# An order written by a model: memory-path transfers, first byte and arrival enter the model up to a given time

## The chip, the cores and the metric

One Trainium2 chip, of which the kernel uses one core. The metric is device time in microseconds of one execution; the median of three runs of the kernel before is 947.36 us (947.36 to 947.47).

## The reference

Two layers on 256 positions of width 1024, all in float32. Each layer is

```python
h = rmsnorm(x, ffn1_norm[i])
x = x + 0.5 * swiglu(h, ffn1_w_gate[i], ffn1_w_up[i], ffn1_w_down[i])      # 1024 -> 2816 -> 1024
h = rmsnorm(x, mix_norm[i])
q_s, k_s, v_s, q_m = jnp.split(h @ w_in[i], ...)                           # 1024 -> 3*768 + 256
k_m, v_m = jnp.split(rmsnorm(mem, mem_norm[i]) @ w_mem_kv[i], 2, axis=-1)  # 256 memory rows
o_m = memory_attention(rmsnorm(q_m), rmsnorm(k_m), v_m)                    # 4 heads of 64
o_s = chunked_rel_attention(...) if i % 2 == 0 else diff_attention(...)    # 12 heads, or 6 double ones
x = x + jnp.concatenate([o_s, o_m], axis=-1) @ w_out[i]
h = rmsnorm(x, ffn2_norm[i])
x = x + 0.5 * swiglu(h, ffn2_w_gate[i], ffn2_w_up[i], ffn2_w_down[i])
```

So there are four feed-forward parts and two attention parts: feed-forward, attention, feed-forward (layer 0), then the same for layer 1.

## The kernel before, in words

**The arithmetic.** TensorE works on fp32r operands. To keep float32 accuracy each operand is split in a high part (a cast) and a low part (the rest), and each product takes three matmuls: high with high, high with low, low with high (`dense`, L542, L545, L548). Weights come as blocks of 128 x 2048 floats (1 MB) into one of three `raw` buffers. ACT casts them to `hi` (`split_hi`, L367) and DVE subtracts to get `lo` (`split_lo`, L385), into one of four split buffers. Some products use seven products in place of eight, on sums of blocks (`wsum`, L379; the matmul groups `pair_m` and `m`).

**A feed-forward part.** Eleven groups of 256 hidden columns, each with two blocks that hold gate and up columns (`gu` banks), then eleven blocks of the down projection (`acc` banks). After a group `evac` takes it out: ACT's silu (L728), DVE's product (L731) and a 32 x 32 transpose into `hb` (L739). The rest of the transpose is a trip through DRAM: `hd` from `hb` (L745) and back as `hr` (L751), both issued on SyncE. Then `hr` is split to `ht`, the left operand of the down projection.

**Attention.** The input projection in five column groups (`pj` banks), a norm of each head (`qkn`, L1049), TensorE transposes (`qktp`), scores (`S`), softmax, transposes of the probabilities, values (`AV`), and the output projection. Layer 0 also holds, ahead of it, the projection of the memory rows. These rows go through DRAM too (`through_dram`, L1064, and `from_dram`, L1069: tiles `md` and `mr`), as do the memory keys (`kd` and `kr`).

**What sets the order.** No scheduler reorders anything: each engine runs its instructions in the order in which the program emits them. The order comes from a small model, `Flow`, that runs while the program is written. It has a clock `now`, which a matmul of 512 columns moves by `T_MM` = 0.216 us, and a time at which each of ACT, DVE and GpSimd gets free. Pieces of work are generators that yield the model time, or the condition, at which they may go on. When TensorE's next matmul needs something, the model lets time pass until it is there, and emits on the way whatever other work has become ready. Semaphores on the chip still hold each instruction until its operands are there, so a wrong model costs time, and nothing else.

Three generators bring in the weights, in the background. `loader` issues a block's transfers on SyncE's queue as soon as a `raw` buffer is free in the model (L321), and writes down when it takes the block to have arrived. `split_hi` emits the casts of a block after that time, when ACT has nearly no backlog in the model or TensorE needs the block; `split_lo` does the same on DVE and frees the `raw` buffer. `dma_free` is the model's time at which the queue has finished: it grows by 3.0 per block, and by small amounts for the first loads of x and the small parameters. In the kernel before no other transfer is in it. The trips through DRAM have fixed delays of their own (3.0, 2.0 and 6.5 around `hd` and `hr`).

Of the kernel before, what the change touches and what calls it, by code (L numbers as in the profile page):

```python
# [167 lines left out]
def kernel(  # L168
# [13 lines left out]
    flow = Flow()  # L182
# [28 lines left out]
    def load_x(tb, hf):  # L211
        nc.sync.dma_start(out=xs[tb][:, hf * 512:(hf + 1) * 512],
                          in_=x[0, tb * P:(tb + 1) * P, hf * 512:(hf + 1) * 512])
# [86 lines left out]
    dma_free = [3.25]  # L300
    slow = [0.0]
    LAT = 1.5
    at = [0]

    def add_raw(parts):
        chunks.append(Chunk(parts))
        return chunks[-1]

    def add_chunk(parts, uses=8, w=1):
        return Item([add_raw(parts)], uses, w)  # L310

    def loader():
        for i, c in enumerate(chunks):
            yield lambda: raw_left[0] > 0
            raw_left[0] -= 1
            c.raw = wraw.tile([P, 2048], F32, tag="raw", name=f"raw{i}")
            dma_free[0] = max(dma_free[0], flow.now)
            n = len(c.parts)
            lat = LAT + slow[0] if i > 1 else 0.6
            for j, (dst, src) in enumerate(c.parts):  # L320
                (nc.scalar if i == 0 and j == 1 else nc.sync).dma_start(out=dst(c.raw), in_=src)  # L321
                dma_free[0] += 3.0 / n
                if i < 2 and j % 2:
                    for q in range((j - 1) * 4 // n, (j + 1) * 4 // n):
                        c.block[q] = dma_free[0] + lat
                if i == 0 and j == 1:
                    table_hint(AF.Silu)
                    load_x(1, 0)
                    dma_free[0] += 0.75
            c.arrive = dma_free[0] + lat  # L330
            c.block = [t or c.arrive for t in c.block]
            if i == 1:
                for tb in range(2):
                    load_x(tb, 1)
                    dma_free[0] += 0.75
            if i > 4 and late_done[0] < len(late_loads):
                dst, src = late_loads[late_done[0]]
                late_done[0] += 1
                nc.sync.dma_start(out=dst, in_=src)
                dma_free[0] += 0.3  # L340
# [371 lines left out]
    def ffn(l, nm, xt, gc_next):  # L712
# [6 lines left out]
        def evac(g, ps, end, gives=None):  # L719


            hb = None
            for tb in range(2):
                yield lambda: end[tb] is not None and xt.rt[tb] is not None
                yield end[tb]
                yield g2.has(3)
                sil = g2.take([P, 256], F32, "sil")
                nc.scalar.activation(sil, ps[tb][:, 0:256], AF.Silu, scale=xt.r[tb])  # L728
                yield flow.act(256)
                h = g2.take([P, 256], F32, "h")  # L730
                nc.vector.scalar_tensor_tensor(out=h, in0=ps[tb][:, 256:512], scalar=xt.r[tb], in1=sil,  # L731
                                               op0=ALU.mult, op1=ALU.mult)
                t = flow.dve(256, 0.06)
                g2.give()
                (gives or (banks, banks))[tb].give()
                if hb is None:
                    hb = g2.take([P, 4, 2, 2, 32], F32, "hb")
                yield t
                nc.vector.transpose(out=hb[:, :, tb].rearrange("p b f j -> p f b j"),  # L739
                                    in_=h.rearrange("p (f b i) -> p f b i", f=2, b=4))  # L740
                t = flow.dve(256, 0.05)
                g2.give()
            yield t
            hd = dram.tile([4, 32, 4, P], F32, tag="hd", name="hd")
            nc.sync.dma_start(out=hd.rearrange("a i b x -> (a i) (b x)"), in_=hb.rearrange("p b t f j -> p (b t f j)"))  # L745
            yield flow.now + 3.0
            g2.give()
            yield flow.now + (8.0 if (l, nm) == (0, 1) and g < NG - 3 else 2.0)
            yield g2.has()
            hr = g2.take([P, 4, P], F32, "hr")  # L750
            nc.sync.dma_start(out=hr, in_=hd.rearrange("a i b x -> (i b) a x"))  # L751
            yield flow.now + 6.5
            src = hr.rearrange("p a (c j) -> p c a j", c=4)
            if g in sv:
                yield from seven_forms(g, src)
                return
            yield g4.has()
            ht = g4.take([P, 2, 4, P], F32R, "ht")
            hi, lo = (ht[:, i].rearrange("p c (a j) -> p c a j", a=4) for i in range(2))
            nc.scalar.copy(out=hi, in_=src)  # L760
            yield flow.act(512)
            nc.vector.tensor_sub(lo, src, hi.bitcast(F32))
            t = flow.dve(512)
            g2.give()
            hts[g], htt[g] = ht, t

        def seven_forms(g, src):


            yield lambda: g4.left >= 2 and g2.left >= 4 and (sv.index(g) < 2 or prog[0] >= sv[1])  # L770
            ht = [g4.take([P, 8, P], F32R, "h7") for _ in range(2)]
            sf = g2.take([P, 4, P], F32, "sf")
            s1, s2, s3, s4 = (sf[:, j].rearrange("p (a j) -> p a j", a=4) for j in range(4))
            for op, o, x, y in ((nc.vector.tensor_add, s1, src[:, 2], src[:, 3]), (nc.vector.tensor_sub, s2, s1, src[:, 0]),
                                (nc.vector.tensor_sub, s3, src[:, 0], src[:, 2]), (nc.vector.tensor_sub, s4, src[:, 1], s2)):
                op(o, x, y)
                t = flow.dve(P, 0.06)
            yield t
            view = lambda x: x.rearrange("p c (a j) -> p c a j", a=4)
            parts = ((slice(0, 2), src[:, 0:2], view(ht[0][:, 0:2]), view(ht[1][:, 0:2])),  # L780
                     (slice(2, 3), src[:, 3:4], view(ht[0][:, 2:3]), view(ht[1][:, 2:3])),
                     (slice(3, 7), sf, ht[0][:, 3:7], ht[1][:, 3:7]))
            ts = []
            for js, x, hi, lo in parts:
                nc.scalar.copy(out=hi, in_=x)
                ts.append(flow.act(P * (js.stop - js.start)))
            for (js, x, hi, lo), t in zip(parts, ts):
                yield t
                nc.vector.tensor_sub(lo, x, hi.bitcast(F32))
                t = flow.dve(P * (js.stop - js.start))  # L790
            g2.give(2)
            hts[g], htt[g] = ht, t

        def seven(c, ms):

            flow.until(lambda: hts[c] is not None)
            ht, first, last = hts[c], c == sv[0], c == sv[-1]
            for q, j, m in ((0, 0, 0), (1, 1, None), (2, 6, None), (3, 3, 1), (4, 4, 2), (5, 5, 3), (6, 2, None)):
                ps = ms[m] if m is not None else acc.ps[q // 6][q // 2 % 2 if q < 6 else 0]
                t = dense(ps, ht[0][:, j], ht[1][:, j], lambda: htt[c], dn[c], q,  # L800
                          first and m is not None, last and m is not None)
            g4.give(2)
            return t
# [164 lines left out]
        def down(c, k, tb, hf):  # L968
            sl = slice(hf * 512, (hf + 1) * 512)
            flow.until(lambda: hts[c] is not None)  # L970
            ht = hts[c]
            return dense(acc.ps[tb][hf], ht[:, 0, 2 * tb + k, :], ht[:, 1, 2 * tb + k, :], lambda: htt[c], dn[c], 2 * k + hf,
                         c == 0 and k == 0, k == 1 and c == NG - (2 if split_end and tb == hf == 1 else 1))
# [24 lines left out]
        for c in range(SPLIT):  # L998
            prog[0] = c
            if c in sv:  # L1000
# [3 lines left out]
                t = seven(c, ms)  # L1004
# [15 lines left out]
        for tb in range(2):  # L1020
            flow.spawn(finish(acc, tb, nxt, gc_next, True, (l, nm) == (0, 1)))
            for hf in range(2):
                for c in range(SPLIT, NG - (split_end and tb == hf == 1)):
                    for k in range(2):
                        t = down(c, k, tb, hf)
                if split_end and tb == hf == 1:
                    t = end_sums(t)
# [4 lines left out]
    def table_hint(func):  # L1032
        nc.scalar.activation(dummy, dummy, func)
        flow.act(1, 1.3)
# [27 lines left out]
    def through_dram(src, tag, n):  # L1062
        d = dram.tile([4, 32, 4, P], F32, tag=tag, name=tag, bufs=n)
        nc.sync.dma_start(out=d.rearrange("a i b x -> (a i) (b x)"), in_=src.rearrange("p b t k j -> p (b t k j)"))  # L1064
        return d

    def from_dram(d, name):
        r = g2.take([P, 4, 2, 2, 32], F32, name)
        nc.sync.dma_start(out=r.rearrange("p a t k j -> p a (t k j)"), in_=d.rearrange("a i b x -> (i b) a x"))  # L1069
        return r  # L1070

    def turn_blocks(dst, src):
# [777 lines left out]
```

## Time and profile before

| | |
|---|---|
| median of three runs | 947.36 us |
| the profiled execution | 947.91 us |
| span in its profile | 946.1 us, so 1.8 us lie around it |
| TensorE matmuls (PE) busy | 940.1 us, 99% |
| VectorE (DVE) busy | 830.1 us, 88% |
| ScalarE (ACT) busy | 590.6 us, 62% |
| GpSimd (POOL) busy | 110.2 us, 12% |
| transfers | 206.13 MB, mean 218 GB/s |
| granted TensorE clock | 1.0 |

All times in views of the trace are microseconds from the span's start, and an L with a number is a line of the kernel. PE is TensorE's matmuls, PEld its weight loads, SPq SyncE's queue. A name such as `lo<-raw,hi` is out<-in by the program's tile names. A wait is shown as who waited, then `<-`, then what ended the wait.

### The profile page before, as it was taken

To read this page: it belongs to the slowest core of one execution; us is meant where nothing else is said; L and a number is where in the kernel's file an instruction comes from. 1 tells how busy PE (TensorE), PEld (TensorE's weight loads), DVE (VectorE), ACT (ScalarE), POOL (GpSimd) and SP (SyncE) were. 2 spreads that over 40 slices of the span, in tenths; PEclk is the share of its full clock that TensorE was granted. 3 is DMA by queue.
4 is the path that set the end of the run, shared out by engine and by line. 5 is a ranking of instruction groups with operands and counts; after the bars stand their busy time and mean duration, and the time that the engine had idled before them with its cause. 6 is when DMAs were issued, how large, how long until landed. Compare 5 with 4: busy or idle time off the path is not lost. (4 is left out here: it accounts for less than half of the span.)

```text
span 946.1 us, 13322 instructions
## 1 busy us (share of the span) xinstructions
PE 940.1 (99%) x4456; PEld 773.6 (82%) x4456; DVE 830.1 (88%) x1501; ACT 590.6 (62%) x1126; POOL 110.2 (12%) x160
## 2 busy tenths in 40 slices
PE   9999999999999999999999999999999999999998
PEld 7888888887878888888888888888887788888887
DVE  6989988889787879979889899796999899998995
ACT  6656666677686746647545656563777765655671
POOL 1000038732220000000000000000334100000000
PEclk9999999999999999999999999999999999999999
DMA  9878799788524476887846679775642367589561
GB/s 294 272 228 252 231 324 315 241 263 260 178 90 146 150 250 210 265 287 225 269 146 214 210 237 286 242 249 176 202 130 75 130 222 223 188 251 333 185 220 47
DMA packets 172574, 206.13 MB, mean 218 GB/s; under 512 B 10265, under 2 KB 147290, under 8 KB 172506
## 3 DMA queue, kind: packets, MB, share of 16 engines
q1 hardware_dynamic: 169498, 202.92, 66.9%
q10 hardware_dynamic: 3008, 2.37, 0.8%
q8 instruction: 35, 0.57, 0.3%
q14 instruction: 33, 0.27, 0.1%
HBM read 190.04 MB, written 15.20 MB: 217 GB/s over the span
## 5 line engine op out<-in xcount | busy, mean ns | idle before, releaser
L367 ACT CAST hi<-raw 128x512 fp32r<-128x512 f32 (+1 forms) x466 | 335.6, 770 | 157.3 <-DMA raw<-in_ffn_w_up_dram 53.1
L385 DVE TENSOR_TENSOR lo<-raw,hi 128x512 fp32r<-128x512 f32 (+1 forms) x466 | 393.0, 878 | 28.7 <-ACT hi L367 28.2
L542 PE MATMUL gu<-hi,xh 128*128 128x512 f32 x528 | 206.1, 390 | 0.0
L548 PE MATMUL gu<-hi,xl 128*128 128x512 f32 x528 | 206.0, 390 | 0.0
L545 PE MATMUL gu<-lo,xh 128*128 128x512 f32 x528 | 206.0, 390 | 0.0
L545 PEld LDWEIGHTS gu<-lo,xh 128*128 128x128 f32 x528 | 99.4, 188 | 20.9 <-DVE lo L385 0.4
L542 PEld LDWEIGHTS gu<-hi,xh 128*128 128x128 f32 x528 | 99.6, 189 | 20.5
L548 PEld LDWEIGHTS gu<-hi,xl 128*128 128x128 f32 x528 | 99.4, 188 | 20.6
L548 PE MATMUL acc<-hi,ht 128*128 128x512 f32 x270 | 105.6, 391 | 0.0
L542 PE MATMUL acc<-hi,ht 128*128 128x512 f32 x270 | 105.1, 389 | 0.0
L545 PE MATMUL acc<-lo,ht 128*128 128x512 f32 x270 | 105.1, 389 | 0.0
L367 ACT CAST hi<-wsum 128x512 fp32r<-128x512 f32 x83 | 49.0, 620 | 42.4 <-DVE wsum L379 36.5
L545 PE MATMUL pj<-lo,xh 128*128 128x512 f32 x160 | 63.9, 399 | 0.0
L548 PE MATMUL pj<-hi,xl 128*128 128x512 f32 x160 | 63.8, 399 | 0.0
L542 PE MATMUL pj<-hi,xh 128*128 128x512 f32 x160 | 63.5, 397 | 0.0
L585 POOL TENSOR_TENSOR xr<-v,nhalf 128x1 f32<-128x1 f32 x12 | 9.7, 810 | 427.4 <-DVE v L583 427.4
L545 PEld LDWEIGHTS acc<-lo,ht 128*128 128x128 f32 x270 | 50.7, 188 | 10.6
L548 PEld LDWEIGHTS acc<-hi,ht 128*128 128x128 f32 x270 | 50.7, 188 | 10.4
L542 PEld LDWEIGHTS acc<-hi,ht 128*128 128x128 f32 x270 | 50.7, 188 | 10.3
L385 DVE TENSOR_TENSOR lo<-wsum,hi 128x512 fp32r<-128x512 f32 x83 | 53.7, 678 | 0.0
L728 ACT ACTIVATE sil<-gu,xr 128x256 f32<-128x256 f32 x72 | 33.8, 469 | 21.1 <-PE gu L548 19.6
L585 POOL TENSOR_TENSOR hf<-v,nhalf 128x8 f32<-128x8 f32 (+1 forms) x20 | 33.2, 1659 | 83.2 <-DVE v L583 74.1
(244 smaller groups left out, 1531.7 us busy)
## 6 DMA issues: line engine op xcount, KB each, us to landing
raw<-in_ffn_w_down_dram SPq DMA_DIRECT2D x176, 256.0 KB, 4.5
raw<-in_ffn_w_gate_dram SPq DMA_DIRECT2D x82, 512.0 KB, 4.7
raw<-in_ffn_w_up_dram SPq DMA_DIRECT2D x82, 512.0 KB, 5.2
raw<-in_w_in_dram SPq DMA_DIRECT2D x32, 512.0 KB, 4.9
hd<-hb SPq DMA_DIRECT2D x44, 256.0 KB, 4.9
hr<-hd SPq DMA_DIRECT2D x44, 256.0 KB, 4.9
raw<-in_w_out_dram SPq DMA_DIRECT2D x8, 1024.0 KB, 4.9
raw<-in_w_mem_kv_dram SPq DMA_DIRECT2D x4, 1024.0 KB, 8.5
```

Source lines behind the costliest of these rows:

```text
L367: nc.scalar.copy(out=it.part(0, q, w), in_=src())
L385: nc.vector.tensor_sub(it.part(1, q, w), src(), it.part(0, q, w).bitcast(F32))
L542: nc.tensor.matmul(out=ps, lhsT=xh, rhs=wh, start=start, stop=False)
L545: nc.tensor.matmul(out=ps, lhsT=xh, rhs=wl, start=False, stop=False)
L548: nc.tensor.matmul(out=ps, lhsT=xl, rhs=wh, start=False, stop=stop)
L585: nc.gpsimd.tensor_tensor(out=dst, in0=v[:, :n], in1=nhalf[:, :n], op=ALU.pow)
L728: nc.scalar.activation(sil, ps[tb][:, 0:256], AF.Silu, scale=xt.r[tb])
```

## The change

While the model's clock is below `FULL` = 600:

- the issue of `hd`, `hr` and of the trips of memory rows and memory keys now moves `dma_free`: to 1.7 after now if the queue is idle (the time to the first byte), and 0.8 further (`carry`);
- a weight block starts on the queue 1.7 after its issue at the earliest, in place of at once;
- a weight block counts as arrived 1.9 after its last byte's time, in place of 1.5 (the first two blocks keep their 0.6).

From 600 on the model is as before. No instruction of the kernel is changed; only the order in which they are emitted can be.

```diff
+    FULL = 600.0
+
+    def carry(t):
+        if flow.now < FULL:
+            dma_free[0] = max(dma_free[0], flow.now + 1.7) + t
...
-            dma_free[0] = max(dma_free[0], flow.now)
+            dma_free[0] = max(dma_free[0], flow.now + (1.7 if flow.now < FULL else 0.0))
             n = len(c.parts)
-            lat = LAT + slow[0] if i > 1 else 0.6
+            lat = (1.9 if flow.now < FULL else LAT) + slow[0] if i > 1 else 0.6
...
             nc.sync.dma_start(out=hd.rearrange("a i b x -> (a i) (b x)"), in_=hb.rearrange("p b t f j -> p (b t f j)"))
+            carry(0.8)
             yield flow.now + 3.0
...
             nc.sync.dma_start(out=hr, in_=hd.rearrange("a i b x -> (i b) a x"))
+            carry(0.8)
             yield flow.now + 6.5
...
     def through_dram(src, tag, n):
         d = dram.tile([4, 32, 4, P], F32, tag=tag, name=tag, bufs=n)
         nc.sync.dma_start(out=d.rearrange("a i b x -> (a i) (b x)"), in_=src.rearrange("p b t k j -> p (b t k j)"))
+        carry(0.8)
         return d

     def from_dram(d, name):
         r = g2.take([P, 4, 2, 2, 32], F32, name)
         nc.sync.dma_start(out=r.rearrange("p a t k j -> p a (t k j)"), in_=d.rearrange("a i b x -> (i b) a x"))
+        carry(0.8)
         return r
```

## The prediction

> **What bounds the kernel now.** I read four views in this order: the page's busy times, the stages, the waits, then single stretches. First the busy times of the engines (share of the span, instructions), and the groups that split weights (out<-in, count, then busy and mean ns).
>
> ```profile
> span 946.1 us, 13322 instructions
> PE 940.1 (99%) x4456; PEld 773.6 (82%) x4456; DVE 830.1 (88%) x1501; ACT 590.6 (62%) x1126; POOL 110.2 (12%) x160
> ...
> L367 ACT CAST hi<-raw 128x512 fp32r<-128x512 f32 (+1 forms) x466 | 335.6, 770 | 157.3 <-DMA raw<-in_ffn_w_up_dram 53.1
> L385 DVE TENSOR_TENSOR lo<-raw,hi 128x512 fp32r<-128x512 f32 (+1 forms) x466 | 393.0, 878 | 28.7 <-ACT hi L367 28.2
> ...
> L367 ACT CAST hi<-wsum 128x512 fp32r<-128x512 f32 x83 | 49.0, 620 | 42.4 <-DVE wsum L379 36.5
> ...
> L385 DVE TENSOR_TENSOR lo<-wsum,hi 128x512 fp32r<-128x512 f32 x83 | 53.7, 678 | 0.0
> ```
>
> TensorE is busy nearly all the time. Its matmul ends are modelled, so busy is not yet proof. The stages, cut where first feed-forward, layer-0 attention, second, third feed-forward, layer-1 attention and last feed-forward begin, say where it is idle.
>
> ```profile
> core 0: us, PE busy (x) PEld busy (x) DVE busy (x) ACT busy (x) POOL busy (x), PEclk, DMA share, GB/s
> 7.00:195.00 188.00, 188.00 (x829) 155.18 (x828) 166.72 (x281) 121.43 (x217) 52.05 (x103) 1.00 0.85 272
> 195.00:311.00 116.00, 115.50 (x679) 93.59 (x678) 95.83 (x252) 83.01 (x201) 20.27 (x14) 1.00 0.58 184
> 311.00:488.00 177.00, 177.00 (x790) 146.59 (x789) 157.07 (x254) 105.86 (x174) 2.02 (x3) 1.00 0.70 223
> 488.00:664.00 176.00, 176.00 (x786) 145.76 (x785) 155.90 (x253) 103.64 (x173) 1.12 (x2) 1.00 0.72 230
> 664.00:768.00 104.00, 103.60 (x582) 83.08 (x581) 95.75 (x204) 74.03 (x196) 32.02 (x28) 1.00 0.47 151
> ...
> sum 934.00, PE 933.10 PEld 767.50 DVE 827.01 ACT 587.75 POOL 108.95; mean PE 155.52 PEld 127.92 DVE 137.83 ACT 97.96 POOL 18.16
> ```
>
> From 7 to 941 us TensorE stands idle for 934.00 - 933.10 = 0.90 us in all: 0.50 in layer-0 attention, 0.40 in layer-1 attention, nothing in a feed-forward part. Next, whether a busy TensorE is a full one. In these stretches (TensorE alone; the count holds the matmul that begins at either end) 24 matmuls of 512 columns run from start to start.
>
> ```profile
> core 0: us, PE busy (x), PEclk, DMA share, GB/s
> 102.61:108.05 5.44, 5.44 (x25) 1.00 0.98 337
> 170.61:176.05 5.44, 5.44 (x25) 1.00 0.83 263
> 181.49:186.93 5.44, 5.44 (x25) 1.00 0.38 134
> 454.04:459.48 5.44, 5.44 (x25) 1.00 0.50 176
> ```
>
> Always 5.44 / 24 = 0.2267 us, whether transfers keep the queues 98% or 38% busy. That pitch is the floor of the stream; short gaps cannot hide in it. So the order has 0.90 us left to win, before any of it is known to be winnable.
>
> Then who waits. The first block is TensorE's waits (total, times, longest); the second the casts that wait for weights; the third SyncE's queue between 340 and 380 us.
>
> ```profile
> PE warm L1778 <- POOL ident masks.py:199: 1.4, 1, 1.4
> PE qktp L578 <- DVE qkn L1049: 0.4, 1, 0.4
> PE S L1487 <- ACT PT L1501: 0.2, 1, 0.2
> ```
>
> ```profile
> ACT hi L367 <- DMA raw<-in_ffn_w_up_dram: 53.1, 32, 5.0
> ...
> ACT hi L367 <- DMA raw<-in_ffn_w_down_dram: 14.4, 9, 2.3
> ...
> ACT hi L367 <- DMA raw<-in_w_in_dram: 8.9, 6, 2.6
> ```
>
> ```profile
> SPq L321 <- DVE lo L385: 14.5, 5, 5.4
> SPq L751 <- DMA hd<-hb: 11.1, 2, 6.4
> ```
>
> The casts do meet late transfers (53.1 + 14.4 + 8.9 = 76.4 us), so the order's clock is too early about them; but no such lateness reaches TensorE, whose waits after the warm-up are 0.4 and 0.2 us.
>
> **The change, part by part.** No instruction is removed or added: `carry` only moves the order's own clock of the queue. What can move is the place of casts (ACT), subtractions (DVE) and DMA issues (SyncE) in their queues. The rows that price its numbers, from the page's DMA issues (KB each, median us to landing):
>
> ```profile
> raw<-in_ffn_w_gate_dram SPq DMA_DIRECT2D x82, 512.0 KB, 4.7
> raw<-in_ffn_w_up_dram SPq DMA_DIRECT2D x82, 512.0 KB, 5.2
> ...
> hd<-hb SPq DMA_DIRECT2D x44, 256.0 KB, 4.9
> hr<-hd SPq DMA_DIRECT2D x44, 256.0 KB, 4.9
> ```
>
> *First byte and arrival.* On an idle queue the order believed that a 1 MB block is usable 3.0 + 1.5 = 4.5 us after its issue; now 1.7 + 3.0 + 1.9 = 6.6. Measured, each half takes 4.7 to 5.2 us, and the second is issued about 0.5 later, so some 5.7. The model goes from 1.2 too early to 0.9 too late. On a busy queue the 1.7 vanishes in the maximum and only 0.4 is left.
>
> *h, memory rows, keys as traffic.* Each 256 KB leg adds 0.8; at the 337 GB/s of the first stretch above 256 KB is 0.78 us, so the size is true. A gate and up block then costs the order 3.0 + (two legs per two blocks) 0.8 = 3.8 us against 24 x 0.216 = 5.2 us of its TensorE time: its queue still has room, and no backlog builds up. So a block is planned later by 0.4 to 2.1 us, by 3.7 if both legs stand just ahead. The few memory, key and value transfers do the same in layer-0 attention alone.
>
> *What a later split costs.* It lets other work go first. Other work is (590.6 - 335.6 - 49.0) / 946.1 = 22% of ACT's time and (830.1 - 393.0 - 53.7) / 946.1 = 41% of DVE's. Over 3.7 us that is 0.8 + 1.5 = 2.3 us per block, over 2.1 us it is 1.3. It is hidden as long as split weights wait for TensorE longer than that. The thinnest such cover in the steady part is in the second feed-forward part:
>
> ```profile
> 367.72 2.35 DVE L385 TENSOR_TENSOR lo<-raw,hi 128x1024 fp32r<-128x1024 f32 x2
> ```
>
> ```profile
> 371.31 0.39 PE L545 MATMUL gu<-lo,xh 128*128 128x512 f32 x1
> ```
>
> These two subtractions make one block's low parts; the first ends about half of the 2.35 in, at 368.9, and TensorE first uses it at 371.31: cover 2.4 us. A typical later split (1.3) fits, the extreme one (2.3) just fits; elsewhere cover is larger, so the cost is taken as 0. If the cover is gone, each further microsecond is one of TensorE's.
>
> *What it can win.* Casts stand less often before work that is ready; DVE and ACT then reach evacuations earlier. The one place where this touches TensorE is layer-0 attention (DVE row, then TensorE's):
>
> ```profile
> 226.47 0.68 DVE L385 TENSOR_TENSOR lo<-raw,hi 128x512 fp32r<-128x512 f32 x1
> 227.07 0.74 DVE L1049 SCALAR_TENSOR_TENSOR qkn<-pj,xr,hf 128x512 f32<-128x512 f32 x1
> ```
>
> ```profile
> 227.96 0.30 PE L578 MATMUL qktp<-flip,qkn 128*128 128x128 f32 x1 [0.43 <-DVE qkn L1049]
> ```
>
> A weight subtraction of 0.68 stands right ahead of the head norm for which TensorE then waits 0.43. If that subtraction goes later, the norm is 0.6 earlier and the 0.43 is gone; next would be the S matmul's 0.2. Equally another split can land ahead of another norm (+0.6). Bounds of this term: -0.9 (all idle gone) to +1; I take half of the 0.43, -0.2.
>
> *SyncE's queue.* Loads (L321), hd (L745) and hr (L751) share it. A buffer that the order frees later may issue its load behind an hr instead of ahead of it, and an hr waits up to 6.4 us for its hd, with the loads behind it. Its two ends are 0 and 6.4 - 2.4 = 4.0 us; at 0, since an hr already stands ahead of loads today with no wait on TensorE.
>
> *The limit of 600.* 600 of the order's time at 0.216 a matmul is about 600 x 0.2267 / 0.216 = 630 us of the trace, inside the third feed-forward part (488 to 664). By then blocks wait for free split buffers, not for transfers, so what follows should keep its order; cost 0.
>
> Sum: the profiled execution took 947.91, 1.8 around its span of 946.1, and lies 0.55 above the median of 947.36. Its span becomes 946.1 - 0.2 = 945.9, its time 947.7, and the median 947.36 - 0.2 = **947.2**.
>
> A rule to weigh against it: the Trainium skill, "TensorE: Matmul & The Clock Gate", Back-to-back issue gap, gives N/2.4 + 2.5 ns for isolated warm matmuls, 215.8 ns at 512 columns. By that every 512-column matmul here loses 10.9 ns to something, about 40 us in all. The trace speaks against an order as its cause, the pitch being 226.7 with much and with little traffic; what would follow is rival three.
>
> **The rivals.** *One, nothing that matters moves:* the casts keep their places relative to TensorE's needs. For it: zero idle in every feed-forward part. 947.4, inside measurement.
>
> *Two, slower: a load goes behind a blocked hr.* Place: 340 to 380 us, where SyncE already stands 6.4 us on hd and the cover is 2.4. It decides once a block comes more than 2.4 us later; at the full 6.4 TensorE waits 4.0, giving 951.4; over 0.2% (1.9 us) needs a delay of 4.3. Against it: loads there wait as long (5.4) for a free buffer, which an hr ahead of them mostly overlaps. By the same page's Part 1 (the HAM clock gate) an idle window of some 3.4 us halves the clock until it has been busy as long, an estimate of 1.7 us more, 953.1; no wait in the steady part of this trace is long enough to show it.
>
> *Three, faster: the pitch itself falls.* If it hung on neighbours' traffic or on ACT's and DVE's order, a fall of 1% would be worth 0.01 x 933 = 9 us, 938. The four equal stretches speak against it.
>
> **How the numbers follow.** 0.2%, 1.9 us, is about what a measurement of this kernel can tell from no change. Forecast (small waits shift, 946.4 to 948.6) 0.68; rival one 0.13; rival two, with its kin in the attention stages (several norms delayed), 0.15 over the bound; rival three and any other gain over 1.9 us 0.04. So faster 0.04, same 0.81, slower 0.15. The low end is all idle gone, 947.36 - 0.9 = 946.4; the high end takes in rival two from its start to a wait of about 2.1 us, 949.5; some 0.17 is left outside.
>
> **What the profile after would show.** Right: TensorE's idle from 7 to 941 us stays under 2 us and its pitch at 0.2267; the casts' 76.4 us for weights falls, since other work now stands ahead of them. The qktp wait shrinks or another norm takes its place. Wrong: TensorE waits on `lo` in a feed-forward part, with an hr before its load on SyncE; or the last two stages differ in order.

## The result and the profile after

The changed kernel takes **949.09 us** in the median of 17 runs (948.33 to 950.36); the kernel before, beside it, 947.47 (947.10 to 947.99, 17 runs). That is 1.62 us more, a ratio of 1.0017 with a 95% interval of 1.0011 to 1.0024. The forecast was 947.2 and no change; the time lies inside its range of 946.4 to 949.5, on the slow side.

The profiled executions understate this: after's took 948.63 (0.46 under its median), before's 947.91 (0.44 above its own). So the two traces differ by 0.7 us of the 1.6, and the size has to come from medians. First TensorE's waits, then the stages cut as before, both of the kernel after.

```profile
PE warm L1788 <- POOL ident masks.py:199: 1.4, 1, 1.4
PE qktp L584 <- DVE qkn L1057: 0.6, 1, 0.6
PE gu L551 <- DVE lo L391: 0.5, 1, 0.5
PE S L1497 <- ACT PT L1511: 0.3, 1, 0.3
```

```profile
7.00:195.00 188.00, 187.51 (x828) 153.98 (x827) 166.02 (x281) 121.21 (x216) 45.99 (x91) 1.00 0.84 271
195.00:311.00 116.00, 115.36 (x676) 93.17 (x675) 95.61 (x252) 83.03 (x200) 25.39 (x26) 1.00 0.58 185
311.00:488.00 177.00, 177.00 (x790) 146.53 (x789) 156.95 (x254) 106.36 (x174) 2.02 (x3) 1.00 0.69 223
488.00:664.00 176.00, 176.00 (x786) 145.73 (x785) 155.75 (x252) 103.89 (x172) 0.86 (x1) 1.00 0.72 230
664.00:768.00 104.00, 103.53 (x582) 83.30 (x581) 94.95 (x206) 74.12 (x197) 32.27 (x28) 1.00 0.46 149
...
sum 934.00, PE 932.40 PEld 765.94 DVE 825.72 ACT 589.05 POOL 108.01; mean PE 155.40 PEld 127.66 DVE 137.62 ACT 98.18 POOL 18.00
```

TensorE's idle time between 7 and 941 us went from 0.90 to 934.00 - 932.40 = 1.60. In the first feed-forward part it is 0.49 (a wait at 8 us, in the first block, which comes and goes between kernels whose order there is the same); in layer-0 attention 0.64, one wait of `qktp` for a head norm, where before had 0.50.

Idle time alone misplaces the loss. Both traces hold 4456 matmuls, so the start of the n-th can be compared from one to the other. At 14 us the kernel after is 0.28 us ahead, in spite of its wait at 8 us. It loses 0.36 between 62 and 130 us, in the first feed-forward part, and 0.63 from 195 to 311 us, in layer-0 attention; everywhere else together it is under 0.05. These two places are what has to be explained.

GpSimd (the fifth figure) is the loudest difference in the stage rows: in layer-0 attention its busy time went from 20.27 us to 25.39. A chain on GpSimd that used to be over by 195 us now reaches into attention.

### The profile page after: what moved, and what is told of

Same layout as the page of the kernel before. It is cut to its first block, busy times and chain, and to the rows that moved or that the text cites. A ratio compares the mean times of both kernels' runs of the same rounds, so it can differ in the third digit from the quotient of the medians.

```text
span 946.8 us, 13315 instructions
## 1 busy us (share of the span) xinstructions
PE 940.2 (99%) x4456; PEld 772.8 (82%) x4456; DVE 828.9 (88%) x1501; ACT 592.0 (63%) x1126; POOL 109.2 (12%) x160
## 5 line engine op out<-in xcount | busy, mean ns | idle before, releaser
L373 ACT CAST hi<-raw 128x512 fp32r<-128x512 f32 (+1 forms) x466 | 333.9, 770 | 140.6 <-DMA raw<-in_ffn_w_up_dram 39.6
```

Of the source, the lines that this page charges most:

```text
L373: nc.scalar.copy(out=it.part(0, q, w), in_=src())
```

## The experiments

Eleven kernels ran. The table puts beside each median two figures of its trace: VectorE's busy time from 195 to 211 us, and TensorE's idle time from 195 to 311 (layer-0 attention). "Ratio" is to the kernel before in the same runs, with its 95% interval; the median of before was 947.47 beside after, and 947.76, 947.58 and 947.52 beside the other three groups of kernels.

| kernel | median us | ratio | VectorE busy, 195 to 211 | TensorE idle, 195 to 311 |
|---|---|---|---|---|
| before | 947.47 | | 13.40 | 0.50 |
| after | 949.09 | 1.0017 (1.0011 to 1.0024) | 13.26 | 0.64 |
| first feed-forward part only | 949.80 | 1.0024 (1.0015 to 1.0033) | 11.17 | 2.06 |
| after the first part only | 947.42 | 0.9999 (0.9990 to 1.0008) | 14.29 | 0.00 |
| arrival numbers only | 949.28 | 1.0019 (1.0011 to 1.0028) | 12.48 | 1.65 |
| traffic only | 947.32 | 0.9996 (0.9988 to 1.0005) | 13.75 | 0.00 |
| after, h planned later | 948.94 | 1.0014 (1.0005 to 1.0023) | 12.44 | 1.37 |
| after, small loads earlier | 948.48 | 1.0010 (1.0001 to 1.0018) | 14.27 | 0.00 |
| before, angles late | 948.99 | 1.0016 (1.0008 to 1.0025) | 12.72 | 2.33 |
| after, short angle chain | 947.25 | 0.9994 (0.9985 to 1.0004) | 15.35 | 0.00 |
| after, no sine tables | 947.85 | 1.0007 (0.9998 to 1.0015) | 14.91 | 0.00 |
| after, both repairs | 948.02 | 1.0005 (0.9996 to 1.0014) | 13.77 | 0.00 |
| traffic only, short chain | 949.78 | 1.0025 (1.0014 to 1.0036) | 12.76 | 1.33 |

### Which part, and where

Two cuts of the change, each both ways. By the order's clock, whose first feed-forward part ends at 177.8 (the other kernel has the lower bound in the loader's two lines too):

```diff
-    FULL = 600.0
+    FULL = 177.8                       # first feed-forward part only
...
-        if flow.now < FULL:
+        if 177.8 <= flow.now < FULL:   # the other kernel: all but the first part
```

> The changed model holds only up to 177.8 of the order's clock, the end of the first feed-forward part; from there on the model of before. Theory A (the loss lies in the first feed-forward part: the cover of the split weights is gone between 70 and 125 us, and TensorE waits for lo by amounts that differ from run to run): 948.7, +1.2 +- 0.4 over before, runs spread over about 2 us, cover below 1 us near 110 us in the trace. Theory B (the loss lies in layer-0 attention, where norms come later): 947.5, as before, runs within 1 us.

> The reverse: the changed model holds only from 177.8 to 600 of the order's clock, and the first feed-forward part is ordered as before. Theory A: 947.5 +- 0.4, runs within 1 us, no wait for lo in the first feed-forward part. Theory B: 948.5 to 949, with 0.5 us or more of added waits between 195 and 311 us.

And by what is modelled: in one kernel `carry` does nothing, in the other the loader keeps its old numbers:

```diff
 def carry(t):
     if flow.now < FULL:
-        dma_free[0] = max(dma_free[0], flow.now + 1.7) + t
+        pass                           # arrival numbers only
...
-            dma_free[0] = max(dma_free[0], flow.now + (1.7 if flow.now < FULL else 0.0))
+            dma_free[0] = max(dma_free[0], flow.now)     # traffic only
...
-            lat = (1.9 if flow.now < FULL else LAT) + slow[0] if i > 1 else 0.6
+            lat = LAT + slow[0] if i > 1 else 0.6
```

> The later arrival alone (1.7 to the first byte, 1.9 after the last), and h, memory rows and keys not counted as traffic. If the arrival numbers cause the loss (they set weights behind the casts of hr in the first feed-forward part): 949.0, as the full change, cover below 1 us near 110 us. If the traffic causes it: 947.5.

> h, memory rows and keys counted as traffic, with the weights' arrival as before (nothing to the first byte, 1.5 after the last). If the arrival numbers cause the loss: 947.5 +- 0.4 and a cover of 2 us or more all through the first feed-forward part. If the traffic causes it: 949.

Measured: 949.80 and 947.42; 949.28 and 947.32. The loss is made by the order of the first feed-forward part and, taking the two cuts together, by the two arrival numbers there, 1.7 and 1.9 (no kernel has these in the first part alone, and none tells the 1.7 from the 1.9). Counting h, memory rows and keys as traffic costs nothing. Neither theory is right as it stands: A names the part that makes the loss, but its 948.7 was too low, and the loss is paid where B looked. Of the kernel with the first part alone, TensorE's idle rows:

```profile
214.12 0.50 PE L551 MATMUL pj<-lo,xh 128*128 128x512 f32 x1 [0.16 <-DVE lo L391]
223.36 0.44 PE L584 MATMUL qktp<-flip,qkn 128*128 128x128 f32 x2 [1.69 <-DVE qkn L1057]
```

A change of the order up to 177.8 on the order's clock, some 195 us of the trace, is paid for at 214 to 224 us. Two things can carry it there, and both stand in the traces.

*Theory C, cover.* Split weights of the first feed-forward part are ready later against TensorE's need. The subtractions of one block near 107 us and its first use, of the kernel before and then after:

```profile
106.21 2.35 DVE L385 TENSOR_TENSOR lo<-raw,hi 128x1024 fp32r<-128x1024 f32 x2
```

```profile
111.00 0.39 PE L545 MATMUL gu<-lo,xh 128*128 128x512 f32 x1
```

```profile
109.67 2.35 DVE L391 TENSOR_TENSOR lo<-raw,hi 128x1024 fp32r<-128x1024 f32 x2
```

```profile
110.94 0.50 PE L551 MATMUL gu<-lo,xh 128*128 128x512 f32 x1
```

```profile
110.94 0.19 PEld L551 LDWEIGHTS gu<-lo,xh 128*128 128x128 f32 x1 [0.44 <-DVE lo L391]
```

The first of the two subtractions ends half of the 2.35 in: 107.4 before, 110.85 after. Cover went from 3.6 us to 0.1, and the weight load of that matmul has already waited 0.44 (the last row).

*Theory S, sines.* `loader` issues one of the small parameter loads behind each weight block. Later blocks carry the positions and frequencies later, and GpSimd computes the rotary angles from them, in a chain of some 95 short instructions. GpSimd's waits, before and then after:

```profile
POOL pos_f L1233 <- DMA pos_i<-in_positions_dram: 85.8, 1, 85.8
```

```profile
POOL pos_f L1243 <- DMA pos_i<-in_positions_dram: 93.8, 1, 93.8
```

The conversion of the positions, for which these waits stand, starts 5.5 us later (109.60 before, 115.09 after), and the last instruction of the chain ends 9.9 us later (194.42 and 204.33). So the delay grows on the way, where the chain waits for a cast on ScalarE (134.05 and 137.77) and shares GpSimd with other work; the load is its first link, not all of it. At the end of the chain ScalarE takes two sines, behind one table load, and then an exponential for lambda, behind another. Before, then after:

```profile
194.67 1.28 ACT L1281 ACT_TABLE_LOAD   x1
...
196.90 1.28 ACT L1321 ACT_TABLE_LOAD   x1
```

```profile
202.59 1.66 ACT L373 CAST hi<-raw 128x512 fp32r<-128x512 f32 x3 [3.09 <-DMA raw<-in_w_in_dram]
...
206.04 1.28 ACT L1291 ACT_TABLE_LOAD   x1
...
207.76 1.28 ACT L1331 ACT_TABLE_LOAD   x1
```

Before, the table loads ran ahead of ScalarE's wait for a late block of the input projection (1.79 us, up to 202.98). After, ScalarE waits 3.09 us for that block and loads tables behind it, nearer to the head norms.

### Sines or cover

Sines early, cover left thin: one of the five constants of the angle reduction is left out, which makes GpSimd's chain shorter.

```diff
-        for piece in range(5):
+        for piece in range(4):
```

> The changed kernel with the rotary angles reduced in four pieces instead of five (one of the five constants of the reduction is left out), so that GpSimd's chain is about 8 us shorter. The order of every engine is that of the changed kernel up to the sines; ScalarE's two sines with their table loads and the lambda exponential move forward, in front of the second key/value square of the memory instead of behind the third. Theory S (the late sines cost the time: 3.2 us of ScalarE's work fall into the crowded stretch ahead of the first head norms): 947.2 to 947.8, ratio to before 0.9995 to 1.0005, TensorE's wait of qktp for qkn gone or under 0.3 us, table loads near 195 to 199 us. Theory C (the thin cover of the split weights in the first feed-forward part costs it): that cover stays thin, 948.7 to 949.5, ratio 1.0015 to 1.002, and the wait for qkn stays.

Sines late, cover left whole, on the kernel before:

```diff
+        yield flow.now + 9.0
         nc.gpsimd.tensor_copy(pf, pi)
```

> The kernel before, none of the change in it; the rotary angles' chain on GpSimd is started 9 us later on the order's clock, so that the sines with their table loads stand behind the third key/value square, as in the changed kernel. Theory S: 948.6 to 949.6, ratio 1.001 to 1.002, and TensorE waits 0.5 to 1.7 us for qkn in layer-0 attention although the split weights of the first feed-forward part keep their cover (thinnest 3.6 to 6.7 us where the changed kernel has 0.1 to 1.3). Theory C: 947.4, ratio 1.000, no wait for qkn above 0.4 us.

Cover back, sines left late:

```diff
-            yield flow.now + 6.5
+            yield flow.now + (9.5 if (l, nm) == (0, 1) else 6.5)
```

> The changed kernel with the order's wait for the read-back of h raised from 6.5 to 9.5 us in the first feed-forward part alone, so that the casts of h go behind the split weights of the next block again. Theory C: the cover of gu blocks 8 and 9 comes back to 3 us or more, and the time to 947.4. Theory S: the cover comes back as well, but the sines stay behind the third key/value square (their place in ScalarE's order is that of the changed kernel), so the time stays at 948.6 to 949.5 with a wait for qkn of 0.5 to 1.7 us.

Small loads earlier, nothing left out:

```diff
-            if i > 4 and late_done[0] < len(late_loads):
+            if i > 3 and late_done[0] < len(late_loads):
```

> The changed kernel with the small parameter loads starting one weight block earlier (after block 3 instead of 4), so that positions and frequencies land earlier and GpSimd's chain starts earlier; the sines then stand two casts behind their place in the kernel before. The computation is whole. Theory S: 947.2 to 947.9, no wait for qkn above 0.4 us. Theory C: the order of the first feed-forward part keeps the new arrival numbers and its thin cover, so 948.6 to 949.5.

Measured: 947.25, 948.99, 948.94, 948.48. The first two are a swap. With early sines the loss is gone although the cover at that block is still 0.1 us (GpSimd's chain ends at 189.0, 15 us earlier than in the changed kernel, where about 8 was expected). With late sines the kernel before is nearly as slow as the changed one, though its cover at that block is 2.6 us and no weight load waits for split weights between 10 and 195 us. Its TensorE idle rows:

```profile
222.37 0.44 PE L578 MATMUL qktp<-flip,qkn 128*128 128x128 f32 x2 [1.33 <-DVE qkn L1049]
229.74 0.41 PE L578 MATMUL qktp<-flip,qkn 128*128 128x128 f32 x2 [1.00 <-DVE qkn L1049]
```

These two waits make 2.33 us, where 0.5 to 1.7 was expected, and they do not come from the table loads alone. With the sines moved, a cast on ScalarE that VectorE needs (`xh`) stands behind a late weight, and VectorE waits 2.7 us for it; for the exponential it waits 0.5. So this kernel shows that a later chain alone costs as much, by way of ScalarE's queue; that the table loads are the cost it does not show.

The third agrees in time and wait (1.37 us, table load at 204.9), though it brought the cover back only in part (gu blocks 8 and 9 have 1.1 to 3.7 us, 3 or more was expected). The fourth is half a miss: its table load comes at 194.5 and no norm is late, as expected, yet 0.9 us over before is left where at most 0.3 was expected.

### The table loads alone

The narrowest form: the sines become copies, so the rotary tables hold wrong values, and every engine keeps the order of the changed kernel: in the two traces TensorE's, VectorE's and GpSimd's instructions stand in the same order, and ScalarE's too but for the two table loads (the exponential then needs none).

```diff
-        nc.scalar.activation(sn, acc, AF.Sin, scale=S2PI)
-        nc.scalar.activation(cs, a, AF.Sin, scale=S2PI)
+        nc.scalar.activation(sn, acc, AF.Copy, scale=S2PI)
+        nc.scalar.activation(cs, a, AF.Copy, scale=S2PI)
```

> The changed kernel with the two sines replaced by copies (the rotary tables then hold angles and not sines). Every engine's order is that of the changed kernel; the only difference is that ScalarE loses two table loads of 1.28 us each at 206 to 209 us. Theory S in its narrow form (the loss is ScalarE's 2.56 us of table loads in the crowded stretch ahead of the head norms): TensorE's wait for qkn goes, 947.2 to 948.0, what is left above before being the 0.4 us of the thin cover in the first feed-forward part. If instead it is the late writing of the rotary tables on VectorE, or another part of the changed order, the time stays at 948.6 to 949.5 and the wait for qkn at 0.5 us or more.

Measured 947.85, 0.33 over the kernel before beside it, where the changed kernel stood 1.62 over; and no wait for `qkn`. VectorE's rows show the path, of the changed kernel and then of this one.

```profile
207.77 0.19 DVE L1301 SCALAR_TENSOR_TENSOR ropeC<-gqk,ropew 128x32 f32<-128x32 f32 x1 [0.50 <-ACT ropew L1292]
...
209.29 0.16 DVE L1333 SCALAR_TENSOR_TENSOR nlam<-le 128x1 f32<-128x1 f32 x1 [1.22 <-ACT le L1331]
...
221.70 0.73 DVE L1057 SCALAR_TENSOR_TENSOR qkn<-pj,xr,hf 128x512 f32<-128x512 f32 x1
```

```profile
207.56 0.15 DVE L1333 SCALAR_TENSOR_TENSOR nlam<-le 128x1 f32<-128x1 f32 x1
...
219.93 0.74 DVE L1057 SCALAR_TENSOR_TENSOR qkn<-pj,xr,hf 128x512 f32<-128x512 f32 x1
```

VectorE stands 0.50 us for the sines and 1.22 for the exponential, 1.72 in all. From there to its first head norm it works without a wait in both kernels, and the norm starts 1.77 us later (221.70 against 219.93). Without the table loads the norm ends at 220.67 and TensorE takes it at 221.81, so TensorE had 1.1 us to spare; it waits the 0.64 that is left. By the starts of the matmuls, whose order is the same in both, it falls 0.81 us behind at this place; idle time counts from modelled ends.

The two stretches around the head norms show the same as sums. Columns as in the stages; first the changed kernel, then this one, then the kernel before with late angles.

```profile
195.00:211.00 16.00, 16.00 (x72) 13.27 (x71) 13.26 (x29) 11.89 (x23) 10.00 (x17) 1.00 0.87 280
211.00:227.00 16.00, 15.36 (x70) 12.46 (x69) 15.90 (x35) 11.59 (x24) 5.41 (x3) 1.00 0.86 272
```

```profile
195.00:211.00 16.00, 16.00 (x72) 13.23 (x72) 14.91 (x32) 10.38 (x23) 10.10 (x17) 1.00 0.87 280
211.00:227.00 16.00, 16.00 (x75) 13.22 (x74) 15.70 (x36) 10.60 (x21) 5.41 (x3) 1.00 1.01 316
```

```profile
195.00:211.00 16.00, 16.00 (x72) 13.24 (x72) 12.72 (x28) 11.49 (x22) 10.26 (x18) 1.00 0.76 236
211.00:227.00 16.00, 14.67 (x68) 11.88 (x67) 14.56 (x33) 11.19 (x24) 4.13 (x3) 1.00 0.93 306
```

From 211 to 227 us VectorE is busy for 15.90 of 16.00 in the changed kernel: it has no room to catch up. What it doesn't do from 195 to 211, because it waits for ScalarE's tables and casts, comes out as a late head norm. The table of all kernels goes with it: every other one with 13.3 us or less in that column stands 0.64 or more in attention, every one with 13.75 or more stands 0.00, and before lies between, though only 0.14 from after.

Two waits of VectorE near that stretch make the difference, and only one of them is for tables. For tables it stands 1.7 us in after, 1.8 with the arrival numbers only and 1.9 with h planned later. For a cast `xh` behind a late weight it stands 3.5 with the first part only (and 1.2 for tables), 2.7 in before with late angles and 2.4 with traffic only and the short chain. In the six kernels that stand 0.00 in attention neither is over 1.2. ScalarE itself is busy for only 11.9 of 16 there; its idle time is no room either, since it is spent waiting for weights with the rest of its queue behind.

The kernel without tables also excludes GpSimd's late work as such: in it GpSimd is as busy in that stretch (10.10 us against 10.00), and TensorE never waits. The Trainium skill, "GPSIMD Engine Reference", Key points, says that GpSimd shares its SBUF interfaces with VectorE; if that costs anything here, it is not what moved the time.

### What is left of cover, and a faster version

Both repairs at once:

```diff
-            yield flow.now + 6.5
+            yield flow.now + (9.5 if (l, nm) == (0, 1) else 6.5)
...
-            if i > 4 and late_done[0] < len(late_loads):
+            if i > 3 and late_done[0] < len(late_loads):
```

> The changed kernel with both repairs: the small loads one weight block earlier (sines early) and the order's wait for the read-back of h 9.5 instead of 6.5 in the first feed-forward part (casts of h behind the split weights). With the small loads alone the time was 948.48. If its remainder of 0.9 us over the kernel before is the thin cover in the first feed-forward part (0.66 us of waits for lo in its profile): 947.3 to 947.8 here. If the remainder is something later in the kernel: 948.2 to 948.8, with TensorE never idle for lo between 62 and 125 us.

Measured 948.02, under the 948.48 of the small loads alone and a little above what was expected. But it doesn't settle the remainder, as the second repair again failed to bring the cover back. What TensorE's idle time hides, its weight loads show: a matmul that waits inside the stream is drawn longer (0.50 for 0.39 us at 110.94), and the wait stands on PEld (0.44 there). PEld's waits for split weights from 10 to 195 us, of the kernel after, and of the one with the small loads earlier:

```profile
PEld gu L551 <- DVE lo L391: 0.4, 1, 0.4
PEld pair_m L551 <- DVE lo L391: 0.2, 1, 0.2
```

```profile
PEld gu L551 <- DVE lo L391: 0.8, 1, 0.8
```

With both repairs it is 0.8 as well, with the short chain 0.4 and 0.3; before and the kernel without tables have none. That last one has the order of the changed kernel all through the first part, so thin cover is a price that one execution pays and another doesn't. By the starts of the matmuls it costs, between 62 and 130 us, 0.36 in after, 0.48 with the short chain, 0.67 with the small loads earlier and with both repairs, and 0.01 without tables. In the two kernels with 0.67 it is the only place behind 14 us where the trace loses on before: a sign that their remainder is cover, but of one execution each.

The candidate for a faster version took the harmless half of the change and the short chain:

```diff
-            dma_free[0] = max(dma_free[0], flow.now + (1.7 if flow.now < FULL else 0.0))
+            dma_free[0] = max(dma_free[0], flow.now)
...
-            lat = (1.9 if flow.now < FULL else LAT) + slow[0] if i > 1 else 0.6
+            lat = LAT + slow[0] if i > 1 else 0.6
...
-        for piece in range(5):
+        for piece in range(4):
```

> The part of the change that cost nothing (the rows of h, memory and keys counted as traffic; the first byte and the later arrival not) with the angle chain of four pieces. It is the candidate for a version faster than both. TensorE's idle time from 7 to 941 us is 0.9 us in the kernel before and under 0.5 in the traffic part alone, so no more than 0.5 us can be won: 946.9 to 947.4, ratio 0.9993 to 0.9999. If a part of the order behind the sines gets worse instead: 947.6 or more.

Measured 949.78, the worst but one, where 946.9 to 947.4 was expected. Its table load for the sines is at 181 us, earlier than in any other kernel, and that is no better. ScalarE's row and VectorE's:

```profile
197.23 0.62 ACT L373 CAST hi<-raw 128x512 fp32r<-128x512 f32 x1 [3.07 <-DMA raw<-in_w_in_dram]
```

```profile
198.40 0.69 DVE L660 TENSOR_TENSOR xl<-y,xh 128x512 fp32r<-128x512 f32 x1 [2.36 <-ACT xh L656]
```

ScalarE stands 3.07 us before a cast whose weights are late, the cast `xh` that VectorE needs is queued behind it, and VectorE stands 2.36. VectorE's 16 us hold 12.76 of work, and TensorE waits for `qkn` again (1.1 us in two waits). With the tables at 197 us, in the traffic part alone, ScalarE's wait for that weight is 1.07. So it is not "early sines are good"; what the traces have in common is whether VectorE is kept fed from 195 to 211 us. That the late cast is the cost here is read from this one trace; no run varies it alone. No kernel that ran beats the kernel before by more than its interval: the best three, 947.25 to 947.42, have intervals that hold 1.

## Why the prediction was wrong

**The step that failed is "What a later split costs", taken as 0.** It priced other work that moves ahead of splits by 2.3 us per block at most, against a thinnest cover of 2.4 us in the second feed-forward part. Two things were wrong with it.

*The price had no term for what hangs on the loader.* A later block also carries a later small load, and behind it hang GpSimd's angles, the sines and two table loads. That term is most of the loss: with the tables taken out the changed kernel stands 0.33 over before in place of 1.62, and with the short chain 0.33 under it. (In the traces with and without tables, 0.91 of the difference falls in layer-0 attention, and 0.35, which the edit does not touch, in the cover.) Delaying the chain alone in the kernel before costs 1.41 (948.99 - 947.58 in the same runs), there mostly by a cast that the moved sines leave behind a late weight. The prediction followed what the loader issues for weights, and h beside them, and not these loads.

*The cover was read in the wrong stage.* At the block that the prediction used, in the second part, it grew, from 2.4 to 3.8 us (the first subtraction ends at 368.2, the first use is at 372.01). In the first part, which I never priced, it fell from 3.6 to 0.1 us, more than the 2.3 of the step. This cost 0 to 0.7 us in single profiles; the medians do not separate it from zero (the kernel without tables stands 0.3 above before, its interval holding 1). What part of the 1.62 it is in the median, and of the 0.9 that the kernel with earlier small loads keeps, stays open.

**"What it can win", -0.2 with bounds -0.9 to +1: right place, wrong sign and size.** I named layer-0 attention, the head norm and the chance of work landing ahead of it. I looked for a weight subtraction of 0.6 on VectorE; it was two table loads of 1.28 on another engine, for which VectorE stood 1.72. The part of the change that I had in mind does what I said: without the first part, or with the traffic alone, the wait for `qkn` is gone and the medians are 947.42 and 947.32 (not to be told from before).

**"First byte and arrival": sizes right, and it was the half that mattered.** I found the model 1.2 us too early before and 0.9 too late after, and drew from the second only that splits come later. **h, memory rows, keys: right**, harmless by the run with traffic alone.

**SyncE's queue (0) and the limit of 600 (0): right.** No idle time of TensorE in the second and third feed-forward parts; the last two stages keep 103.53 and 173.00 of TensorE where before had 103.60 and 173.00. Behind 604 us no instruction of TensorE, VectorE, ScalarE or GpSimd stands at another place in its engine's order. Rivals two (a load behind a blocked hr) and three (pitch) did not happen: from 340 to 380 us SyncE waits 10.5 us for hd where it waited 11.1, behind 195 us no weight load waits for split weights, and the two stages without idle time hold 790 and 786 matmuls, as before.

**That the time lies inside the range is luck.** The prediction's own forecast, that small waits shift, ended at 948.6, and 949.09 is past it. The range went on to 949.5 only to take in the start of rival two, which did not happen. Its kin, several late norms in attention, is the nearest that the prediction came to what happened, and it had a chance but no price of its own.

**The marks.** "Idle under 2 us": held (1.60), and was too generous, since 0.7 more idle time went with a loss of 1.62. "The casts' 76.4 us for weights falls": held, but only to 39.6 + 25.9 + 6.3 = 71.8,

```profile
ACT hi L373 <- DMA raw<-in_ffn_w_up_dram: 39.6, 23, 7.0
...
ACT hi L373 <- DMA raw<-in_ffn_w_down_dram: 25.9, 15, 4.2
```

since the largest fell from 53.1 to 39.6 us and the wait for down blocks rose from 14.4 to 25.9. The sum fell and the kernel got slower, so less of this wait was no gain here. "Wrong if TensorE waits on lo in a feed-forward part with an hr before its load": a wait on `lo` came, small and on PEld, at 110.94 us. An hr is in the neighbourhood, on another engine: ScalarE's cast of h, moved ahead of split casts, stood 3.96 us for its hr.

```profile
66.28 0.62 ACT L768 CAST ht<-hr 128x512 fp32r<-128x512 f32 x1 [3.96 <-DMA hr<-hd]
```

That this carries on to the wait 45 us later is not shown: the kernel without tables has the same wait (3.92) and no wait on `lo`. The last mark, "the last two stages differ in order", did not come.

The chance of 0.81 for less than 0.2% came true with 0.17%, at the edge; it was high for a stage whose 0.5 us of idle time already said that a norm there is just in time.

## What to carry to other kernels

When a change delays a background generator, list everything that it issues, the small loads too, and follow each to the engine where it ends. An engine with no idle time behind a deadline sets the price: look which engine is busy 15 of 16 us there, and ask what may keep it waiting in the stretch before; an idle ScalarE that waits in order for a late transfer is no room. A model that is nearer to the truth is not a faster order if the old error hid something, here two table loads, 2.56 us, for which the order's clock counts 0.3 at most (`flow.act(n, 0.3)` for the sines).

## What the runs showed of the hardware

A table load takes 1.28 us and the next activation starts at its end (206.04 + 1.28 = 207.32; it starts at 207.34). ScalarE's delay per load is 1.4 us: from the square ahead of them to the exponential it takes 3.49 us with the two loads (205.56 to 209.05) and 0.65 without (205.72 to 206.37), since activations in a row overlap a little (without loads the square ends at 206.18 and the next one starts at 206.08) and a load does not. The Trainium skill, "ScalarE: Activation LUTs", What ACT_TABLE_LOAD costs, gives 1283 ns, with which the trace agrees, and 1380 ns of drain on top, which it doesn't show: the load begins at 206.04, and the square before it began at 205.56 and took 0.46.

Unexpected was how far single runs of one kernel spread: those of after over 2.0 us, those of before beside it over 0.9. Thin cover is not shown to be the reason: before with late angles, where no weight load waits for split weights from 10 to 195 us, spreads over 2.3.
